# A buffer of its own for two kinds of working values, and a fifth slot in the shared pool

## The chip, the cores and the metric

The kernel runs on one core of one Trainium2 chip. A core has a matrix engine (TensorE, PE in the rows) and three engines for vectors, VectorE (DVE), ScalarE (ACT) and GpSimd (POOL); SyncE (SP) issues most of the loads. Each engine runs its own list of instructions in order; between engines semaphores order the work. Matrix products are written to PSUM, everything else lies in SBUF, the core's on-chip memory. The metric is the time of one execution on the device in microseconds: here 2623.21, the median of three runs (2622.59 to 2624.29).

## The reference, cut to what matters

Two decoder layers over 256 positions of width 2048, in f32. Layer 0 mixes latent attention (MLA) with a gated delta rule (GDN, 8 heads, chunks of 64 positions); layer 1 is a gated linear attention (GLA, 4 heads). After each mixer comes a SwiGLU feed-forward stage. Three pieces matter here:

```python
def rms_norm(x, gain):
    y = xf * lax.rsqrt(jnp.mean(xf * xf, axis=-1, keepdims=True) + EPS)
    return y * gain

# gated delta rule, per chunk of 64:
t_mat = jnp.eye(cs) + lower
sol = lax.linalg.triangular_solve(t_mat, rhs, left_side=True, lower=True, unit_diagonal=True)

# gated linear attention, per chunk of 64:
rel = jnp.exp(jnp.where(causal, b_c[:, :, :, None, :] - b_c[:, :, None, :, :], -jnp.inf))
scores = jnp.einsum('bhid,bhjd,bhijd->bhij', q_c, k_c, rel)
o = rms_norm(o, norm_g) * jax.nn.silu(r)
```

The modulation that stands around every stage is a product with a vector, `silu(c) @ ada_w`.

## The kernel before, in words

Activations are kept transposed: 16 tiles of 128 features by 256 positions (T = 256). Weights are loaded as f32 tiles `raw`; ScalarE casts each to `hi` (`L253`), VectorE subtracts to get `lo` (`L193`), and TensorE adds up products with both parts. These main products go to PSUM tiles `acc`, the small ones of the mixers to `sm`. Products for the modulation (`pa<-araw,sc`, VectorE's `ada`) are spread between them.

The stages in order: input projection with the convolution of the GDN (to about 320 us), MLA and GDN woven into each other (to 560), output projection (to 620), feed-forward 0 (to 1395), projections and heads of the GLA (to 1740), its output projection (to 1856), feed-forward 1 and the final norm. Python generators are woven (`weave`, `braid`) so that work of two kinds alternates in the program; a scheduler of the framework then fixes each engine's order, and a slot that is not free counts in it: an instruction is put where its slot is free. Which slot is free when thus decides the order of all engines.

The pool `tp` has these tags: `tmp`, working values of at most 128 x 512, 4 slots; `sv`, values of a few columns, 12 slots; `ss`, 1 slot, which holds the running sum of squares in `x_square`; `rs`, 1 slot. Those who use `tmp` are many: the steps of MLA and GDN, the squares, the tiles of `h_tile` at a stage's start, and the levels of the GLA.

Four pieces of the program are touched or stand next to what is touched.

`gdn_blocks` solves the 16 x 16 diagonal blocks of a half (4 heads) by substitution on GpSimd: 15 steps, each a product `w` and a subtraction. It then copies the result transposed (`L954`, ScalarE), stores both (`L956`) and loads them rearranged (`L959`). `gdn_local` stores each head's matrix with GpSimd DMAs (`L918`), which stand in the same order as the substitution. `gdn_merge` joins the blocks to 64 x 64, with small products on TensorE and, among others, the copies of `L1015`.

`rstd` gives 1 / rms: logarithm and exponential on ScalarE and a correction on VectorE, with two working values `w` and `y`. It serves the norms of MLA (`mla_rstd`), GDN (`gdn_tail`, 128 x 512), GLA (`gla_pv`), the stage norms (`x_rstd`) and the last one.

`gla_scores` computes a head's scores in eight levels (1 to 128). For each, `prepare` takes a `tmp` slot for the exponents `e` (two subtractions on VectorE, exp on ScalarE) and one for `ke` (product with k), and the product with q goes in place; `prepare` runs one level ahead. TensorE then multiplies the two (`sm<-tmp,tmp`). `gla_pv` multiplies by v, squares the four output tiles (a `tmp` slot each, ScalarE `L203`), sums them by products with ones (`sm<-tmp,cst`) and calls `rstd`.

`h_tile` makes a stage's input: a first step to `tmp` (`L200`), ScalarE's high part, and a second step that gives `d` (`L200`), which TensorE reads.

Of the kernel before, what the change touches and what calls it, by code (L numbers as in the profile page):

```python
# [9 lines left out]
F32 = mybir.dt.float32  # L10
# [9 lines left out]
T = 256  # L20
# [109 lines left out]
class Trunk:  # L130
# [29 lines left out]
        return s.dp.tile(list(shape), dt, tag="d", name=s.nm("d"))  # L160

    def tmp(s, shape=(128, 512), dt=F32):
        return s.tp.tile(list(shape), dt, tag="tmp", name=s.nm("tmp"))

    def sv(s, shape):
        return s.tp.tile(list(shape), F32, tag="sv", name=s.nm("sv"), bufs=12)
# [58 lines left out]

    def rstd(s, out, ss, n, eps=EPS):

        w = s.tmp(out.shape)
        y = s.tmp(out.shape)
        s.act(y, ss, AF.Ln, scale=1.0 / n, bias=s.eps[:out.shape[0]])  # L230
        s.ts(w, ss, -0.5 / n, ALU.mult, -0.5 * eps, ALU.add)
        s.act(y, y, AF.Exp, scale=-0.5)
        s.tt(w, w, y, ALU.mult)
        s.tt(w, w, y, ALU.mult)
        s.stt(out, w, 1.5, y, ALU.add, ALU.mult)
# [697 lines left out]
    def gdn_blocks(s, half):  # L933


        nc = s.nc
        lt = s.d((64, 16, 16))
        nc.gpsimd.dma_start(lt, s.lt[half].rearrange("u (b r) -> (u b) r", b=8)[:, :2048].rearrange(
            "l (j i) -> l j i", i=128)[:, :, :16])
        tr = s.d((64, 2, 16, 16))  # L940
        t = tr[:, 0]
        nc.gpsimd.memset(t, 0.0)
        nc.gpsimd.memset(t.rearrange("l i c -> l (i c)")[:, 0:256:17], 1.0)
        for _ in range(W0):
            yield
        for k in range(15):
            n, m = 15 - k, k + 1
            w = s.tmp((64, 16, 16))[:, :n, :m]
            s.tt(w, lt[:, k, m:].unsqueeze(2).broadcast_to([64, n, m]),
                 t[:, k, :m].unsqueeze(1).broadcast_to([64, n, m]), ALU.mult, nc.gpsimd if SG else None)  # L950
            s.tt(t[:, m:, :m], t[:, m:, :m], w, ALU.subtract, nc.gpsimd if SG else None)
            if k % SK == SK - 1:
                yield
        nc.scalar.copy(tr[:, 1], t.rearrange("l i c -> l c i"))  # L954
        blk = s.drp.tile([2, 64 * 256], F32, name=s.nm("blk"))
        nc.gpsimd.dma_start(blk.rearrange("a (l r) -> l a r", l=64), tr.rearrange("l a i c -> l a (i c)"))  # L956
        s.tc16[half] = s.d((128, 2, 8, 16))
        for a in range(2):
            nc.gpsimd.dma_start(s.tc16[half][:, a], blk[a].rearrange("(u b j i) -> (b j) u i", u=8, b=8, i=16))  # L959
        for _ in range(W1):  # L960
            yield
# [712 lines left out]
```

## Time and profile before

| quantity | value |
|---|---|
| median of three runs | 2623.21 us |
| the profiled execution | 2622.07 us |
| its span in the trace | 2620.3 us |
| TensorE busy | 2552.7 us (97%) |
| VectorE / ScalarE / GpSimd busy | 67% / 46% / 4% |
| mean granted clock of TensorE | 0.983 |
| chain of waits that ended last | TensorE 93%, VectorE 3%, ScalarE 1% |

Busy shares are means over the whole span. TensorE does not have a free share of 3% everywhere: the feed-forward stages have none, and what there is lies at the starts and ends of stages and in the mixers. The granted clock is 1.0 at 2.4 GHz and 0.5 at 1.2; work done at the lower takes about twice as long.

### The profile page before, as it was taken

What the parts mean: (1) busy time and instruction counts of PE and PEld (TensorE: products, weight loads), DVE (VectorE), ACT (ScalarE), POOL (GpSimd) and SP (SyncE); (2) the same over time, 40 slices, a digit from 0 to 9 for tenths busy, and PEclk for the clock granted to TensorE, in tenths of its full rate; (3) what the DMA queues carried; (4) which work ended last, traced back from release to release, by engine and by line L of the source; (5) the groups of instructions that cost most, each with busy time, mean ns of one, the idle gap of its engine ahead of it and who ended that gap; (6) DMA issues with size and microseconds to landing.
All of it is one profiled execution on the core that took longest, in us unless ns stands there. A gap on an engine that the chain in (4) does not pass through costs nothing.

```text
span 2620.3 us, 43320 instructions
## 1 busy us (share of the span) xinstructions
PE 2552.7 (97%) x17914; PEld 2285.0 (87%) x17914; DVE 1768.3 (67%) x2455; ACT 1193.8 (46%) x1809; POOL 97.6 (4%) x154
## 2 busy tenths in 40 slices
PE   8999998999999999999998989999999999999998
PEld 5799876799999999999998878878788888888887
DVE  3667654688778777777778777766655655655555
ACT  3435664445433343334345534564544344444344
POOL 0000014001000000000001000001000000000001
PEclk9999998899999999999999999999999999999999
DMA  9975567675979888878885545435455555555553
GB/s 349 351 290 167 212 251 255 261 286 205 341 276 352 310 312 313 323 298 324 308 326 191 203 166 197 166 120 193 161 190 186 189 191 190 182 191 193 177 193 113
DMA packets 262259, 622.31 MB, mean 237 GB/s; under 512 B 17119, under 2 KB 28012, under 8 KB 241582
## 3 DMA queue, kind: packets, MB, share of 16 engines
q1 hardware_dynamic: 259902, 608.32, 65.5%
q0 software_dynamic: 1968, 11.14, 1.2%
q8 instruction: 141, 2.31, 0.3%
q14 instruction: 56, 0.46, 0.0%
q10 hardware_dynamic: 192, 0.08, 0.0%
HBM read 616.09 MB, written 3.41 MB: 236 GB/s over the span
## 4 chain that ended last, share of the span: by engine, by line
PE 93%; DVE 3%; ACT 1%; DMA 1%; issue 1%; POOL 0%; SPq 0%; DVEq 0%; ACTq 0%; POOLq 0%
PE acc L190 85%; PE sm L190 5%; PE pa L190 2%; DVE lo L193 1%; ACT hi L253 1%; DMA araw<-in_ada_w 0%; DVE ada L200 0%; DVE tmp L193 0%; ACT tmp L203 0%; DVE d L193 0%; DMA d<-in_x 0%; POOL ss L193 0%; DMA d<-in_ada_w 0%; DMA d<-in_norm_g 0%; DVE x L200 0%
## 5 line engine op out<-in xcount | busy, mean ns | idle before, releaser
L190 PE MATMUL acc<-d,hi 128*128 128x256 f32 (+2 forms) x9120 | 2138.9, 321 | 16.4 <-DVE d L200 9.2
L190 PE MATMUL acc<-d,lo 128*128 128x256 f32 x6000 | 1642.8, 283 | 3.2 <-DVE lo L193 3.2
L190 PEld LDWEIGHTS acc<-d,hi 128*128 128x128 f32 (+1 forms) x9120 | 1500.7, 191 | 164.7 <-issue 20.6
L193 DVE TENSOR_TENSOR lo<-raw,hi 128x1024 fp32r<-128x1024 f32 (+2 forms) x801 | 945.2, 1204 | 576.1 <-ACT hi L253 560.6
L253 ACT CAST hi<-raw 128x1024 fp32r<-128x1024 f32 x776 | 786.0, 1047 | 991.6 <-PE acc L190 845.9
L190 PEld LDWEIGHTS acc<-d,lo 128*128 128x128 f32 x6000 | 1138.5, 191 | 30.9 <-DVE lo L193 5.4
L200 DVE SCALAR_TENSOR_TENSOR ada<-araw,sc,ada 128x1024 f32<-128x1024 f32 x240 | 299.8, 1287 | 6.3 <-DMA araw<-in_ada_w 6.2
L200 DVE SCALAR_TENSOR_TENSOR x<-acc,mod,x 128x256 f32<-128x256 f32 x272 | 119.8, 478 | 42.5 <-PE acc L190 41.6
L193 DVE TENSOR_TENSOR d<-acc,d 128x256 f32<-128x256 f32 (+1 forms) x200 | 93.2, 474 | 74.1 <-PE acc L190 52.0
L190 PE MATMUL acc<-hi,d 128*128 128x512 f32 (+1 forms) x320 | 96.0, 379 | 1.3 <-DVE d L193 1.3
L190 PE MATMUL pa<-araw,sc 128*32 128x512 f32 x480 | 75.5, 631 | 3.4 <-DMA araw<-in_ada_w 2.0
L223 ACT CAST d<-d 128x256 fp32r<-128x256 f32 x128 | 48.3, 405 | 53.2 <-DVE d L193 53.1
L193 DVE TENSOR_TENSOR d<-d,d 128x256 fp32r<-128x256 f32 (+1 forms) x155 | 61.2, 420 | 12.0 <-ACT d L223 8.2
L190 PEld LDWEIGHTS acc<-hi,d 128*128 128x128 f32 x320 | 58.5, 191 | 12.4 <-DVE d L193 1.4
L190 PE MATMUL acc<-lo,d 128*128 128x512 f32 (+1 forms) x160 | 59.8, 373 | 0.0
L203 ACT ACTIVATE d<-d 128x256 f32<-128x256 f32 (+1 forms) x94 | 45.5, 489 | 26.4 <-DVE d L200 11.6
L193 POOL TENSOR_TENSOR ss<-ss,tmp 128x256 f32<-128x256 f32 x44 | 49.1, 1115 | 72.1 <-ACT tmp L203 70.2
L193 DVE TENSOR_TENSOR tmp<-d,tmp 128x512 f32<-128x512 f32 x64 | 43.9, 687 | 10.0 <-ACT tmp L203 3.9
L514 POOL COPY ss<-tmp 128x256 f32<-128x256 f32 x3 | 2.6, 880 | 1009.5 <-ACT tmp L203 1009.5
L280 ACT COPY d<-acc 128x256 f32<-128x256 f32 x76 | 27.6, 370 | 26.5 <-PE acc L190 25.3
L203 ACT ACTIVATE d<-tmp,mod 128x256 fp32r<-128x256 f32 x64 | 29.2, 502 | 21.6 <-DVE tmp L200 16.6
L190 PEld LDWEIGHTS sm<-tmp,tmp 128*128 128x128 f32 x240 | 31.8, 193 | 8.1 <-issue 6.4
(215 smaller groups left out, 1100.1 us busy)
## 6 DMA issues: line engine op xcount, KB each, us to landing
raw<-in_ffn_w SPq DMA_DIRECT2D x264, 1024.0 KB, 5.1
araw<-in_ada_w SPq DMA_DIRECT2D x175, 1024.0 KB, 7.2
raw<-in_gla_w_in SPq DMA_DIRECT2D x48, 1024.0 KB, 5.1
raw<-in_ab_w_in SPq DMA_DIRECT2D x30, 1024.0 KB, 4.9
raw<-in_ab_w_out SPq DMA_DIRECT2D x16, 1024.0 KB, 5.3
raw<-in_gla_w_out SPq DMA_DIRECT2D x16, 1024.0 KB, 5.1
raw<-in_ab_w_in SPq DMA_DIRECT2D x20, 512.0 KB, 7.5
araw<-in_ada_w POOLq DMA_DIRECT2D x9, 1024.0 KB, 5.1
```

Of the source, the lines that this page charges most:

```text
L190: s.nc.tensor.matmul(out, lhsT=lhsT, rhs=rhs, start=start, stop=stop)
L193: (eng or s.nc.vector).tensor_tensor(out=out, in0=a, in1=b, op=op)
L200: return s.nc.vector.scalar_tensor_tensor(out=out, in0=a, scalar=sc, in1=b, op0=op0, op1=op1)
L203: s.nc.scalar.activation(out, a, f, **kw)
L223: s.nc.scalar.copy(hl[:, 0], x)
L253: s.nc.scalar.copy(hi[:, :n, :ncol], raw[:, a:a + n, :ncol])
L280: s.nc.scalar.copy(out, ps[:, T:])
L514: s.nc.gpsimd.tensor_copy(s.ss, q)
```

## The change

The pool tag `tmp` gets five slots. The substitution's product `w` takes the one slot of `ss`. In `rstd`, values of T columns put `w` in `ss` and `y` in the output itself; values of up to 8 columns put both in `sv`; the 512-column ones of `gdn_tail` stay with `tmp`. The instructions are the same, but for three loads of ScalarE's function tables (32 before, 29 now).

```diff
     def tmp(s, shape=(128, 512), dt=F32):
-        return s.tp.tile(list(shape), dt, tag="tmp", name=s.nm("tmp"))
+        return s.tp.tile(list(shape), dt, tag="tmp", name=s.nm("tmp"), bufs=5)
+
+    def row(s, shape=(128, T)):
+        return s.tp.tile(list(shape), F32, tag="ss", name=s.nm("ss"), bufs=1)
...
     def rstd(s, out, ss, n, eps=EPS):
 
-        w = s.tmp(out.shape)
-        y = s.tmp(out.shape)
+        n1 = out.shape[-1]
+        w = s.sv(out.shape) if n1 <= 8 else s.row() if n1 == T else s.tmp(out.shape)
+        y = out if n1 == T else s.sv(out.shape) if n1 <= 8 else s.tmp(out.shape)
         s.act(y, ss, AF.Ln, scale=1.0 / n, bias=s.eps[:out.shape[0]])
...
         for k in range(15):
             n, m = 15 - k, k + 1
-            w = s.tmp((64, 16, 16))[:, :n, :m]
+            w = s.row((64, 16, 16))[:, :n, :m]
```

The order of the instructions moves with it, on all engines. Three places follow, each first as it stands before and then as it stands now (lines of the code are 3 or 4 higher now, and the numbers behind names differ by a few).

GpSimd, the last steps of the first half's substitution. `lt` is the DMA that stores a head's matrix; `blk` and the last row are the way of the result. Before:

```order
L193 TENSOR_TENSOR d_4003<-d_4003,tmp_4281 64x3x13
L193 TENSOR_TENSOR tmp_4284<-d_4001,d_4003 64x2x14
L193 TENSOR_TENSOR d_4003<-d_4003,tmp_4284 64x2x14
L193 TENSOR_TENSOR tmp_4287<-d_4001,d_4003 64x15
L918 DMA lt_3935<-d_4314 128x2x128
L193 TENSOR_TENSOR d_4003<-d_4003,tmp_4287 64x15
L956 DMA blk_4346<-d_4003 64x2x256
L959 DMA d_4348<-blk_4346 128x8x16 x2
```

The same steps of GpSimd now, with `ss` in place of `tmp`:

```order
L196 TENSOR_TENSOR d_4001<-d_4001,ss_4279 64x3x13
L196 TENSOR_TENSOR ss_4282<-d_3999,d_4001 64x2x14
L922 DMA lt_3933<-d_4185 128x2x128
L196 TENSOR_TENSOR d_4001<-d_4001,ss_4282 64x2x14
L196 TENSOR_TENSOR ss_4285<-d_3999,d_4001 64x15
L196 TENSOR_TENSOR d_4001<-d_4001,ss_4285 64x15
L960 DMA blk_4344<-d_4001 64x2x256
L963 DMA d_4346<-blk_4344 128x8x16 x2
L922 DMA lt_3933<-d_4312 128x2x128
```

The products are written to `ss`; the store that stood ahead of the last subtraction has gone behind the two DMAs of the result, and the store before it, which stood six steps from the end, stands two steps from it.

ScalarE in the second half. The copy from `d` to `d`, 64 x 256, is the transposed copy of the substitution's result; `tmp<-sm`, 32 x 128 are the copies that TensorE's merge needs. Before:

```order
L1019 COPY d_4447<-d_4442 32x4x32 x2
L1017 COPY d_4445<-d_4442 32x4x32 x4
L1015 COPY tmp_4748<-sm_4739 32x128 x2
L1250 COPY tmp_4761<-acc_4757 128x384
L954 COPY d_4411<-d_4411 64x256
L203 ACTIVATE d_4429<-sm_4798 32x4x32
```

The same stretch of ScalarE now:

```order
L1023 COPY d_4445<-d_4440 32x4x32 x2
L1021 COPY d_4443<-d_4440 32x4x32 x4
L958 COPY d_4409<-d_4409 64x256
L1019 COPY tmp_4746<-sm_4737 32x128 x2
L1254 COPY tmp_4759<-acc_4755 128x384
L1254 COPY tmp_4769<-acc_4765 128x384
L1019 COPY tmp_4780<-sm_4771 32x128 x2
```

The transposed copy has moved from behind the first pair of merge copies to in front of it.

TensorE in the last levels of GLA head 0. `sm<-tmp,tmp` are the products of a level, `acc` the main products. Before:

```order
L190 MATMUL acc_16340<-d_15576,lo_16533 128x256
L190 MATMUL acc_16340<-d_15576,hi_16532 128x512
L190 MATMUL sm_16403<-tmp_16367,tmp_16371 128x128 x4
L190 MATMUL sm_16452<-tmp_16396,tmp_16400 128x128 x4
L190 MATMUL sm_16484<-tmp_16445,tmp_16449 128x128 x2
L190 MATMUL sm_16512<-cst_85,d_15858 128x128
L190 MATMUL sm_16512<-cst_85,d_15866 128x128
L190 MATMUL sm_16512<-cst_85,d_15858 128x128
L190 MATMUL sm_16512<-cst_85,d_15866 128x128
L190 MATMUL sm_16520<-d_15755,d_16061 128x128 x4
L190 MATMUL sm_16536<-cst_85,tmp_15421 128x4 x4
L190 MATMUL acc_16607<-hi_16611,d_15501 128x512
```

TensorE now, around the second last level's products and then around the last level's:

```order
L193 MATMUL acc_16335<-d_15552,lo_16469 128x256
L193 MATMUL acc_16335<-d_15552,hi_16468 128x512
L193 MATMUL sm_16448<-tmp_16392,tmp_16396 128x128 x4
L193 MATMUL acc_16336<-d_15537,lo_16465 128x256
```

On either side of the second last level stand main products. The last level:

```order
L193 MATMUL acc_16333<-d_15567,lo_16529 128x256
L193 MATMUL acc_16333<-d_15567,hi_16528 128x512
L193 MATMUL acc_16333<-d_15572,lo_16529 128x256
L193 MATMUL sm_16480<-tmp_16441,tmp_16445 128x128 x2
L193 MATMUL sm_16508<-cst_85,d_15854 128x128
L193 MATMUL sm_16508<-cst_85,d_15862 128x128
L193 MATMUL sm_16508<-cst_85,d_15854 128x128
L193 MATMUL sm_16508<-cst_85,d_15862 128x128
L193 MATMUL sm_16516<-d_15751,d_16057 128x128 x4
L193 MATMUL acc_16333<-d_15572,hi_16528 128x512
```

Before, three levels and the small products behind them stand in one piece. Now main products stand between: 36 between the third last and the second last of these groups, 15 between the second last and the last, and 25 among and behind the small ones.

ScalarE near the end of the last heads. The copies `d<-sm` bring an output tile, the activation `tmp<-d` squares it, `L280` copies carry gate tiles; the pair of activations between table loads is the logarithm and exponential of 1 / rms. Before:

```order
L203 ACT_TABLE_LOAD
L203 ACTIVATE tmp_18096<-sm_17949,eps_105 128x256
L203 ACT_TABLE_LOAD
L203 ACTIVATE tmp_18096<-tmp_18096 128x256
L1488 COPY d_18119<-sm_18122 128x256
L280 COPY d_18156<-acc_17966 128x256
L280 COPY d_18156<-acc_17967 128x256
L1488 COPY d_18119<-sm_18169 128x256
L280 COPY d_18184<-acc_17968 128x256
L280 COPY d_18184<-acc_17969 128x256
L203 ACTIVATE tmp_18126<-d_18119 128x256
L203 ACTIVATE tmp_18173<-d_18119 128x256
```

The same stretch of ScalarE now:

```order
L206 ACT_TABLE_LOAD
L206 ACTIVATE d_18088<-sm_17943,eps_105 128x256
L206 ACT_TABLE_LOAD
L206 ACTIVATE d_18088<-d_18088 128x256
L1492 COPY d_18112<-sm_18115 128x256
L206 ACTIVATE tmp_18119<-d_18112 128x256
L257 CAST hi_18203<-raw_18201 128x1024
L257 CAST hi_18207<-raw_18201 128x1024
L284 COPY d_18149<-acc_17960 128x256
L284 COPY d_18149<-acc_17961 128x256
L1492 COPY d_18112<-sm_18162 128x256
L206 ACTIVATE tmp_18166<-d_18112 128x256
```

The first square has moved from behind six copies to right behind the first one; the output of 1 / rms is its own working value.

## Rows read from the trace of the kernel before

**Rows 1.** The page, part 1: busy time and share of the span.

```profile
...
PE 2552.7 (97%) x17914; PEld 2285.0 (87%) x17914; DVE 1768.3 (67%) x2455; ACT 1193.8 (46%) x1809; POOL 97.6 (4%) x154
```

**Rows 2.** TensorE's waits: for which engine and line, us in total, times, longest.

```profile
...
PE sm L190 <- ACT tmp L203: 8.8, 5, 4.7
PE sm L190 <- DVE tmp L193: 6.0, 2, 4.2
...
```

**Rows 3.** Timeline of GpSimd in both halves: start, us, operation, [idle before <-releaser].

```profile
...
401.76 0.75 POOL L918 DMA_DIRECT2D lt<-d  x1 [1.38 <-DVE d L193]
...
428.33 0.78 POOL L193 TENSOR_TENSOR tmp<-d,d 64x63 f32<-64x63 f32 x1 [3.33 <-PE acc L1248]
429.19 1.18 POOL L193 TENSOR_TENSOR d<-d,tmp 64x63 f32<-64x63 f32 x1
...
434.58 1.14 POOL L193 TENSOR_TENSOR tmp<-d,d 64x55 f32<-64x55 f32 x1
...
438.45 0.21 POOL L193 TENSOR_TENSOR d<-d,tmp 64x15 f32<-64x15 f32 x1
...
```

**Rows 4.** Timelines of ScalarE and TensorE at the merge of the second half.

```profile
...
437.49 0.54 ACT L1015 COPY tmp<-sm 32x128 f32<-32x128 f32 x2 [3.00 <-POOL d L193]
...
438.69 0.62 ACT L954 COPY d<-d 64x256 f32<-64x256 f32 x1
...
437.80 0.47 PE L190 MATMUL sm<-tmp,d 32*32 32x32 f32 x5 [4.75 <-ACT tmp L1015]
...
```

**Rows 5.** Windows: us, busy PE, PEld, DVE, ACT, POOL; PEclk; DMA share; GB/s.

```profile
...
437.00:447.00 10.00, 8.10 (x51) 5.54 (x52) 3.13 (x5) 5.41 (x16) 3.74 (x9) 0.50 1.02 403
...
1522.00:1529.00 7.00, 5.13 (x27) 4.95 (x26) 2.39 (x5) 1.02 (x3) 0.00 (x0) 0.53 0.41 147
...
1731.00:1738.00 7.00, 6.12 (x20) 5.24 (x21) 4.78 (x13) 5.04 (x11) 0.00 (x0) 0.54 0.18 71
...
```

**Rows 6.** Line 959's issues and landings, and TensorE's transposes for attention.

```profile
...
L959 POOL DMA_DIRECT2D d<-blk x4: 892/915/942, 407.6 to 445.5; - x4
...
DMA to landing us min/median/max: 4.0/5.3/7.5
...
410.02 0.44 PE L1248 MATMUL acc<-cst,tmp 128*128 128x128 f32 x2
...
```

**Rows 7.** Timeline of TensorE in the last levels of GLA head 0.

```profile
...
1515.62 0.39 PE L190 MATMUL acc<-d,hi 128*128 128x512 f32 x1
1515.85 0.28 PE L190 MATMUL acc<-d,lo 128*128 128x256 f32 x1
1515.97 0.39 PE L190 MATMUL acc<-d,hi 128*128 128x512 f32 x1
...
1521.40 1.16 PE L190 MATMUL sm<-tmp,tmp 128*128 128x128 f32 x8 [4.16 <-DVE tmp L193]
1524.43 1.19 PE L190 MATMUL sm<-tmp,tmp 128*128 128x128 f32 x4 [1.87 <-DVE tmp L193]
...
1531.25 0.50 PE L190 MATMUL acc<-hi,d 128*128 128x512 f32 x1 [1.29 <-DVE d L193]
...
```

**Rows 8.** The page, part 5: the casts to `lo` (count, busy, mean ns).

```profile
...
L193 DVE TENSOR_TENSOR lo<-raw,hi 128x1024 fp32r<-128x1024 f32 (+2 forms) x801 | 945.2, 1204 | 576.1 <-ACT hi L253 560.6
...
```

**Rows 9.** Timelines of ScalarE and TensorE at the end of the last heads.

```profile
...
1727.68 0.47 ACT L203 ACTIVATE tmp<-sm,eps 128x256 f32<-128x256 f32 x1
...
1729.79 0.35 ACT L1488 COPY d<-sm 128x256 f32<-128x256 f32 x1
...
1731.36 0.77 ACT L203 ACTIVATE tmp<-d 128x256 f32<-128x256 f32 x2
...
1731.88 1.22 PE L190 MATMUL sm<-tmp,cst 128*128 128x256 f32 x2 [4.68 <-ACT tmp L203]
...
```

**Rows 10.** Timelines of VectorE and TensorE at the start of feed-forward 1.

```profile
...
1858.11 1.67 DVE L200 SCALAR_TENSOR_TENSOR tmp<-x,mod,rs 128x256 f32<-128x256 f32 x4
...
1860.32 0.76 PE L190 MATMUL acc<-d,hi 128*128 128x512 f32 x1 [4.84 <-DVE d L200]
...
```

## The prediction

> **What bounds the kernel now.** I began with the page's first part and the chain of waits: TensorE is busy for 97% of the span, so nearly every step of the chain that ended last is one of its matmuls [rows 1]. Both feed-forward stages are matmuls without a hole, so the change has nothing to win there. What it can win is the idle time of TensorE, 2620.3 - 2552.7 = 67.6 us, and time at half clock. The waits of TensorE come second: 8.8 us are waits for `tmp` from ScalarE's line 203 and 6.0 for `tmp` from VectorE's line 193 [rows 2]. Both name the pool that gets a fifth slot. I then read the timelines around the long waits and, last, windows of the granted clock over what follows each of them.
>
> Four places matter: the substitution of the delta rule (387 to 447 us), the levels of head 0 of the gated linear attention (GLA; about 1495 to 1532), the end of its last heads (1726 to 1738), and the stage boundaries near 622, 1406 and 1858.
>
> **The substitution.** The change moves its 30 products (15 per half) from `tmp` to the one `ss` slot. That slot has no other user in this stage, and product and subtraction alternate on GpSimd, which runs in order, so one slot is enough. In the first half nothing waited for a slot; what it lost there are DMA issues that stand between its steps or just ahead of it: the one at 401.76 alone waited 1.38 us and took 0.75 [rows 3]. In the new order this one stands behind the substitution and the two before it stand behind further steps, so this half ends 2.1 us sooner from the one, and by my estimate up to 4 with the others. In the second half a product waited 3.33 us for a `tmp` slot that TensorE was still reading [rows 3]. That wait goes: the end moves from 438.66 (438.45 + 0.21) to 435.3. TensorE's wait of 4.75 us hangs on this: ScalarE's two copies of line 1015 needed a `tmp` slot that GpSimd's products held until 437.49 [rows 4]. They no longer need it, but in the new order the transposed copy of the whole half (line 954, 0.62 us [rows 4]) stands in front of them, and this one waits for the last subtraction. So the copies start at about 435.3 + 0.7 = 436.0 instead of 437.49, and TensorE at 436.3 instead of 437.80: 1.5 us gained.
>
> How fast the products run bounds this from the other side. Their subtractions and products of some 0.3 us took 1.18 us at 429.19 and 1.14 at 434.58 [rows 3], the first and the last of four slow ones; they cost about 4 x 0.85 = 3.4 us. Freed of these too, the half would end at 431.9 and the wait of 4.75 would be gone almost whole, and with it up to 4 us at half clock (437 to 447: 8.10 us of work at 0.50 [rows 5], half of it lost), 8.8 in all. The Trainium skill, page "GPSIMD Engine Reference", section "1. Specifications", says that GpSimd shares its SBUF interfaces with VectorE and contends with VectorE's instructions that have two SBUF inputs. By that rule the slow steps are not slow by their place and come again wherever VectorE's casts run, so the gain stays at the low end, 1.5; without it, it could be 4.75 and more. I take 2.0, near the low end, because VectorE has the same long operations to do between 426 and 436, and I leave the clock as it is: a wait of about 3 us stays, and the stretches behind waits of 1.87 and 4.68 us are granted 0.53 and 0.54 [rows 5, 7, 9], near the lower of the two levels, 1.2 of 2.4 GHz.
>
> A loss belongs to the same place. TensorE's first merge step of the first head pair moves ahead of attention's transposes that stood at 410.02. It needs the blocks that the line 959 DMAs bring: first issued at 407.6, 4.0 to 7.5 us to land, 5.3 in the median [rows 6]. With the substitution 2.1 to 4 us earlier they land between 407.6 and 413.0, so TensorE waits 0 to 3.0 us there. With the median it is 408.9 to 410.8, at most 0.8, and I take 0.8.
>
> **Head 0 of the GLA.** TensorE waits 4.16, 1.87 and 1.29 us for its last levels, 7.3 us together [rows 7], with nothing between them. Each level takes two slots (the exponent and k times it) and is prepared one level ahead, so four slots are all in use and a level's preparation starts when TensorE has read an older one; meanwhile VectorE and ScalarE have worked off casts, the `lo` casts of 1.20 us [rows 8] among them, in the middle of the chain. In the new order the level steps come ahead of later casts, and TensorE gets main matmuls between the levels: 36 ahead of the second last group, 15 ahead of the last, 25 around the small products behind it. Starts are 0.23 us apart behind a wide one and 0.12 behind a narrow one [rows 7], so these are 36 x 0.175 = 6.3, 2.6 and 4.4 us of work for waits of 4.16, 1.87 and 1.29. The second is not quite safe: two `lo` casts (2 x 1.20 us) now stand between the two steps on VectorE. I count 1.5 us as remaining and 0.8 for what the interleaving loses elsewhere: 5.0 gained. At half clock 1522 to 1529 holds 5.13 us of work at 0.53 [rows 5], about 2.4 us lost; I take 1.5 back. Term: 6.5, bounds 0 (the level chain is as long as before and the filler only moves) and 7.3 + 2.4 = 9.7, more if the dip behind it goes too.
>
> **The last heads.** TensorE waits 4.68 us at 1731.88 for a square [rows 9]. ScalarE does the logarithm at 1727.68, the exponential with table loads between, copies from 1729.79 on and only then the square, at 1731.36 [rows 9]: the squares have to wait until 1 / rms, whose two working values and the four squares share four slots, gives some back. With the working value in `ss`, the result in place and five slots, the square stands right behind the first copy, and TensorE has 32 main matmuls between the former square's product and this one: 16 x 0.23 + 16 x 0.12 = 5.6 us. ScalarE needs 1729.79 + 0.35 - 1727.68 = 2.5 us to the end of the first copy and about 0.4 for the square, so the wait can vanish. I take 3.5 of the 4.68, as other waits of the same chain follow (product, rms, gate, output matmul), and 1.5 of the 2.8 that 6.12 us of work at 0.54 lose [rows 5]. Term: 5.0, bounds 0 and 7.5.
>
> **The boundaries.** With a fifth slot one more first step (`tmp` from `x`) goes ahead of the first second step (`d` from `tmp`) on VectorE at the three boundaries. Four take 1.67 us at 1858.11, 0.40 each, and the wait of 4.84 at 1860.32 ends with the first `d` [rows 10]. Each boundary so loses 0.4: -1.2 together. The other edits (1 / rms of the 8-wide values in `sv`, the in-place result at the boundaries, three table loads fewer on ScalarE, which is idle for more than half the span) are at nothing: VectorE's own chain is as long as before, and matmuls cover the rest.
>
> **Sum.** 2.0 - 0.8 + 6.5 + 5.0 - 1.2 = 11.5 us. The profiled execution took 2622.07 us (span 2620.3), 1.1 below the median; from the median the sum gives 2623.21 - 11.5 = 2611.7 us. All terms at their best: 8.8 + 9.7 + 7.5 - 1.2 = 24.8, 2598.4; all at their worst: 1.5 - 3.0 + 0 + 0 - 1.2 = -2.7, 2625.9.
>
> **Rivals.**
> *The waits move, they do not go* (0.22). The chains of levels and of 1 / rms are as long as before, and TensorE meets the same chain with its main matmuls in another place. For it: in the substitution the new copy in front of line 1015 does just that. Against: in the old order TensorE has no main matmul at all between the last levels. A third of the three gains is 13.5 / 3 - 2 = 2.5 us; when one of the two GLA places gains in full it is 6 to 7: 2616 to 2621, the middle 2619.
> *`tmp` was not the limit* (0.08). The slots come free when wanted and only names change: 2623. Against it stands the 3.33 us wait for a slot.
> *Casts too late* (0.15). In the new order level steps and squares stand ahead of hi and lo casts on in-order engines, and TensorE then starves for weights. A pair of `lo` casts costs 2 x 1.20 = 2.4 us when TensorE arrives before it. If this happens at six pairs in the GLA stage, it is 14.4 us, and with one further stretch at half clock (7 us, half lost) 17.9: 17.9 - 11.5 = 6.4 slower, 2629.6. It decides from five pairs on. For it: two casts now stand between the steps of the second last level. Against: over the whole stage VectorE and ScalarE are far from full, and hi and lo have four slots each.
>
> **Numbers.** Forecast 0.55, rivals 0.22, 0.08, 0.15. A difference of 0.2% (5.2 us) is about what can be told from no change here. Of the forecast 0.53 is faster; of the first rival 0.09 faster and 0.13 the same; the second is the same, 0.08; of the third 0.14 is slower and 0.01 the same. Faster 0.62, same 0.24, slower 0.14. The range is 2602 to 2625: below it are the cases with nearly all best terms, above it most of the third rival.
>
> **What would show it.** Right: no wait of GpSimd for a slot in the second half, its end near 435; TensorE's wait for line 1015's copies at 2 to 3.5 us; in head 0 and in the last heads no wait of TensorE over 2 us, and the stretches of 7 us behind these waits with a granted clock well above the 0.53 and 0.54 of before; boundary waits of 4.7 and 5.2 us. Wrong: a wait of several us for the merge step near 410, or waits for `lo` or `hi` in the GLA stage.

## The result, and the profile after

The changed kernel takes 2592.01 us (median of 4 runs, 2590.08 to 2595.17) against 2623.47 (4 runs, 2622.59 to 2624.29): ratio 0.9881, 95% interval 0.9864 to 0.9898, 31.5 us faster. The forecast was 11.5 us. The direction was right, the size was not, and the time lies far below the stated range.

The profiled execution took 2593.56 us, its span is 2591.4. TensorE's own part of the page:

```profile
...
PE 2538.1 (98%) x17914; PEld 2279.1 (88%) x17914; DVE 1769.3 (68%) x2455; ACT 1188.7 (46%) x1806; POOL 99.0 (4%) x154
...
```

Of the 28.9 us of span, idle time of TensorE makes 67.6 - 53.3 = 14.3, and its busy time 2552.7 - 2538.1 = 14.6 [rows 1]. TensorE's instructions are the same, so the second half is work that went faster. The waits of TensorE in the changed kernel, in the columns of [rows 2]:

```profile
...
PE acc L193 <- DVE d L203: 9.8, 2, 5.1
PE sm L193 <- ACT tmp L206: 3.9, 3, 2.3
...
PE sm L193 <- ACT tmp L1019: 3.2, 1, 3.2
...
```

The waits for VectorE's `tmp`, 6.0 us before, are no longer in the list; those for ScalarE's `tmp` fell from 8.8 to 3.9. To see where the time came from I cut both traces at the same instructions of TensorE and took for each stage its length, TensorE's idle time in it, and the work done while the granted clock was at half (worked out from the records of TensorE and of the clock; us):

| stage (us of before) | before: length, idle, work at half clock | changed | its second profile (e8) |
|---|---|---|---|
| start, 0 to 125 | 121.7, 11.7, 13.7 | 120.5, 12.1, 6.7 | 121.7, 11.9, 12.7 |
| convolution, MLA, delta rule, 125 to 640 | 515.0, 13.7, 27.4 | 505.6, 10.7, 24.7 | 504.7, 12.0, 19.5 |
| start of GLA, 1380 to 1415 | 35.0, 7.0, 5.2 | 34.5, 7.4, 4.1 | 34.6, 7.3, 4.5 |
| GLA with head 0, 1415 to 1690 | 275.0, 8.5, 8.4 | 265.2, 0.0, 3.4 | 263.8, 0.0, 0.0 |
| last heads, 1690 to 1760 | 70.2, 4.7, 5.5 | 60.8, 0.0, 0.0 | 60.8, 0.0, 0.0 |
| start of feed-forward 1, 1850 to 1870 | 20.0, 5.3, 3.4 | 21.1, 5.6, 5.2 | 20.1, 5.6, 3.2 |

The two GLA stages give 9.8 + 9.4 = 19.2 us and the delta rule stage 9.4. Of the 19.2 us, 13.2 are idle time and 5.2 the clock (half of the 13.9 - 3.4 us of work at half clock). How they divide at 1690 is less sure: 16 level products (`sm<-tmp,tmp`, some 1.8 us) stand ahead of this cut in the new order and stood behind it before, so that head 0 gained about 11.6 and the last heads about 7.6. What the places of the prediction look like now, in the order of its terms:

GpSimd's timeline in both halves, in the columns of [rows 3]:

```profile
...
381.65 0.21 POOL L196 TENSOR_TENSOR ss<-d,d 64x15 f32<-64x15 f32 x1 [3.68 <-DMA d<-lt]
...
384.13 0.75 POOL L922 DMA_DIRECT2D lt<-d  x1
...
395.06 0.21 POOL L196 TENSOR_TENSOR d<-d,ss 64x15 f32<-64x15 f32 x1
...
410.97 0.53 POOL L994 MEMSET d<- 128x512 f32 x1 [5.09 <-DVE d L196]
411.46 0.21 POOL L196 TENSOR_TENSOR ss<-d,d 64x15 f32<-64x15 f32 x1
...
427.26 1.12 POOL L196 TENSOR_TENSOR d<-d,ss 64x15 f32<-64x15 f32 x1
...
```

No step waits for a slot. The second half ends at 428.4 instead of 438.7, 10 us sooner and not 3.3: it starts at 411.46 where it began at 420.84 before. The kernel before in the same places:

```profile
...
386.55 0.72 POOL L918 DMA_DIRECT2D lt<-d  x1 [3.44 <-DVE d L193]
387.37 0.23 POOL L193 TENSOR_TENSOR tmp<-d,d 64x15 f32<-64x15 f32 x1
...
402.53 0.23 POOL L193 TENSOR_TENSOR d<-d,tmp 64x15 f32<-64x15 f32 x1
...
420.09 0.53 POOL L990 MEMSET d<- 128x512 f32 x1 [8.68 <-PE acc L190]
...
420.84 0.21 POOL L193 TENSOR_TENSOR tmp<-d,d 64x15 f32<-64x15 f32 x1
...
```

ScalarE and TensorE at the merge, as in [rows 4]:

```profile
...
427.12 1.22 ACT L1021 COPY d<-d 32x128 f32<-32x128 f32 x4
428.41 0.62 ACT L958 COPY d<-d 64x256 f32<-64x256 f32 x1
429.06 0.54 ACT L1019 COPY tmp<-sm 32x128 f32<-32x128 f32 x2
...
```

```profile
...
429.37 0.47 PE L193 MATMUL sm<-tmp,d 32*32 32x32 f32 x5 [3.20 <-ACT tmp L1019]
...
```

TensorE still waits 3.20 us, within the 2 to 3.5 that the prediction gave. Near 410 it does not wait at all. Windows over the places, as in [rows 5]:

```profile
...
429.00:436.00 7.00, 6.63 (x50) 5.99 (x51) 0.57 (x2) 2.19 (x8) 0.64 (x1) 0.52 1.00 391
439.00:449.00 10.00, 9.97 (x61) 7.65 (x61) 3.21 (x9) 3.43 (x13) 0.77 (x2) 0.51 0.61 213
1495.00:1525.00 30.00, 30.00 (x177) 26.44 (x176) 26.70 (x45) 14.80 (x22) 0.53 (x1) 1.00 0.56 184
1690.00:1712.00 22.00, 22.00 (x126) 19.36 (x126) 15.53 (x24) 16.38 (x27) 0.00 (x0) 1.00 0.47 154
...
```

In the third row lie the last levels of head 0, in the fourth the last heads: TensorE is busy without a hole and the clock is 1.00, where it was 0.53 and 0.54 behind the waits. The last levels themselves, as in [rows 7]:

```profile
...
1500.83 1.05 PE L193 MATMUL sm<-tmp,tmp 128*128 128x128 f32 x8
...
1504.27 0.61 PE L193 MATMUL sm<-tmp,tmp 128*128 128x128 f32 x4
...
```

Neither row has a wait in brackets. ScalarE in the last heads, as in [rows 9]:

```profile
...
1695.02 0.48 ACT L206 ACTIVATE d<-sm,eps 128x256 f32<-128x256 f32 x1 [0.97 <-PE sm L193]
...
1697.13 0.35 ACT L1492 COPY d<-sm 128x256 f32<-128x256 f32 x1
1697.52 0.42 ACT L206 ACTIVATE tmp<-d 128x256 f32<-128x256 f32 x1
...
```

From the logarithm to the end of the first square are 2.9 us, as worked out, and TensorE has main products for them. At the boundary the wait grew as forecast, from 4.84 to 5.13 [rows 10]:

```profile
...
1830.04 0.76 PE L193 MATMUL acc<-d,hi 128*128 128x512 f32 x1 [5.13 <-DVE d L203]
...
```

### The profile page after: what moved, and what is told of

It is laid out like the page before. It is cut to its first block, busy times and chain, and to the rows that moved or that the text cites. A ratio compares the mean times of both kernels' runs of the same rounds, so it can differ in the third digit from the quotient of the medians.

```text
span 2591.4 us, 43280 instructions
## 1 busy us (share of the span) xinstructions
PE 2538.1 (98%) x17914; PEld 2279.1 (88%) x17914; DVE 1769.3 (68%) x2455; ACT 1188.7 (46%) x1806; POOL 99.0 (4%) x154
## 4 chain that ended last, share of the span: by engine, by line
PE 94%; DVE 2%; ACT 1%; issue 1%; DMA 1%; POOL 1%; SPq 0%; DVEq 0%; ACTq 0%; POOLq 0%
PE acc L193 86%; PE sm L193 5%; PE pa L193 2%; DVE lo L196 1%; ACT hi L257 1%; POOL ss L196 0%; DVE ada L203 0%; DMA d<-in_x 0%; DMA raw<-in_ab_w_in 0%; DVE tmp L203 0%; DMA araw<-in_ada_w 0%; POOL d L196 0%; DVE x L203 0%; ACT tmp L206 0%; DVE d L196 0%
## 5 line engine op out<-in xcount | busy, mean ns | idle before, releaser
L193 PE MATMUL pa<-araw,sc 128*32 128x512 f32 x480 | 70.6, 617 | 4.1 <-DMA araw<-in_ada_w 2.7
L196 POOL TENSOR_TENSOR ss<-ss,tmp 128x256 f32<-128x256 f32 x44 | 48.3, 1097 | 72.3 <-ACT tmp L206 70.3
L206 ACT ACTIVATE d<-tmp,mod 128x256 fp32r<-128x256 f32 x64 | 28.8, 501 | 19.8 <-DVE tmp L203 14.3
L193 PEld LDWEIGHTS sm<-d,d 32*32 32x32 f32 (+2 forms) x368 | 29.8, 146 | 9.2 <-issue 5.9
## 6 DMA issues: line engine op xcount, KB each, us to landing
raw<-in_ab_w_in SPq DMA_DIRECT2D x20, 512.0 KB, 7.9
```

The costliest lines, as they stand in the source:

```text
L193: s.nc.tensor.matmul(out, lhsT=lhsT, rhs=rhs, start=start, stop=stop)
L196: (eng or s.nc.vector).tensor_tensor(out=out, in0=a, in1=b, op=op)
L206: s.nc.scalar.activation(out, a, f, **kw)
```

## The experiments

Theory A: each part pays at its own place: the fifth slot at head 0 of the GLA, 1 / rms at the last heads, products (with 1 / rms) in the delta rule. Theory B: slots are slots, and any that come free give the whole gain. Theory C: the gain is luck of the whole order. Times are medians; each is compared with the kernel before on the same chip: 2620.17 for the first four, 2619.27 for the next four, 2619.22 for the last three.

**The parts alone.** e1 has only the fifth slot, e2 only the products, e3 only 1 / rms, e4 the last two without the slot.

```diff
 e1
-        return s.tp.tile(list(shape), dt, tag="tmp", name=s.nm("tmp"))
+        return s.tp.tile(list(shape), dt, tag="tmp", name=s.nm("tmp"), bufs=5)
 e2
-            w = s.tmp((64, 16, 16))[:, :n, :m]
+            w = s.row((64, 16, 16))[:, :n, :m]
 e3
+        w = s.sv(out.shape) if n1 <= 8 else s.row() if n1 == T else s.tmp(out.shape)
+        y = out if n1 == T else s.sv(out.shape) if n1 <= 8 else s.tmp(out.shape)
```

> Alone of the change: tmp with five slots; products and working values of 1 / rms stay in tmp. Theory A (each part pays at its own place: the fifth slot at the levels of GLA head 0, 1 / rms at the end of the last heads, products and 1 / rms together in the delta rule): its order on TensorE has main matmuls between the last levels of head 0 (36 and 15) and, by the fifth slot, also 38 ahead of the squares' product of the last heads, so the GLA stage (1408 to 1855 before) is shorter by 17 to 20 us; the delta rule stage, where GpSimd's stores stand as before, by 0 to 3: about 2602. Theory B (any slot that comes free is as good as any other, since one pool serves all): 2592 to 2596, all of the 31 us. Theory C (the gain is the scheduler's luck with the whole order): the stages that change do not answer to the places; 2592 to 2623.

> Alone of the change: the substitution's products in the ss slot; four tmp slots, 1 / rms as before. Theory A: GLA as before to 0.5 us, its waits of 4.2, 1.9, 1.3 and 4.7 us and its half clock unchanged; in the delta rule stage GpSimd's wait of 3.3 us for a slot is gone and TensorE's wait of 4.75 us for the line 1015 copies shrinks (the copies stand ahead of the transposed copy here), but the store that held back the first half still stands in front of it: 3 to 6 us, about 2619. Theory B: 2592 to 2610. Theory C: a change of several us in GLA too.

> Alone of the change: the working values of 1 / rms out of tmp; four slots, products in tmp. Theory A: the waits at head 0 stay (no main matmul between its last levels in this order), the wait of 4.7 us at the last heads goes with its half clock (25 main matmuls ahead of that product): 8 us; in the delta rule stage the first store stands six rows later, so the first half is earlier by 3 to 5, but the wait for a slot in the second half stays: 0 to 4 us. About 2612. Theory B: 2592 to 2600. Theory C: 2600 to 2623.

> All of the change but the fifth slot. Theory A: the waits and the half clock of head 0 stay (11 us that the changed kernel saved), the last heads (8 us) and the delta rule stage (9 us) gain as in the changed kernel: 2604 to 2606. Theory B: 2592 to 2597, since products and working values no longer take slots and four are enough. Theory C: no relation to the places.

| run | us, ratio (95%) | 125 to 640: length, idle, work at half clock | 1415 to 1690 | 1690 to 1760 |
|---|---|---|---|---|
| before | - | 515.0, 13.7, 27.4 | 275.0 | 70.2 |
| e1 slot | 2603.80, 0.9943 (0.9927 to 0.9960) | 514.7, 13.7, 20.4 | 263.7 | 60.7 |
| e2 products | 2611.41, 0.9964 (0.9952 to 0.9976) | 500.6, 8.0, 5.5 | 278.3 | 70.3 |
| e3 1 / rms | 2611.12, 0.9964 (0.9952 to 0.9976) | 512.0, 14.4, 28.1 | 277.7 | 61.7 |
| e4 both | 2619.28, 0.9991 (0.9982 to 0.9999) | 512.2, 9.1, 33.1 | 277.7 | 60.8 |

In GLA this is Theory A, with one correction. Head 0's stage is shorter by 11 us with the fifth slot and not at all without it; the products leave its waits as they were (in e2 TensorE's waits there are 4.16 and 1.86), though its stage is 3.3 us longer in e2, with 17.6 us of work at half clock for 8.4 before. The last heads gain 8.5 to 9.5 with the slot alone or with 1 / rms alone: either is enough, so of the change one would have done there. That the GLA stages answer to the parts speaks against C there; e1 with 16.4 of 31.5 us speaks against B (its runs reach from 2600.14 us, at a granted clock of 0.990, to 2612.70, at 0.986).

In the delta rule stage the parts do not add up, and two expectations failed by it: e2 came out 8 us below the 2619 expected, e4 13 us above 2604 to 2606. The products alone save 14.4 us there, more than the whole change; with 1 / rms besides (e4) only 2.8. The difference is mainly the clock. In e2, ScalarE's merge copies come before the end of the substitution, TensorE's wait is 0.64 us instead of 4.75, and the clock stays full; e4 has a stretch at half clock of 25 us:

```profile
...
420.00:450.00 30.00, 29.27 (x378) 21.43 (x379) 16.26 (x33) 18.39 (x55) 15.93 (x38) 1.00 0.81 299
...
```

```profile
...
451.00:476.00 25.00, 24.39 (x238) 16.00 (x238) 10.13 (x21) 6.48 (x21) 0.00 (x0) 0.52 0.49 177
...
```

The first row is e2, the second e4; in [rows 5] the same stage of before had 0.50 over 10 us. Of e4's 12 runs (2612.05 to 2621.95) the profiled one is the fastest, so its median is 7 us above what the table accounts for. The granted clock over the whole run was 0.985 in the profiled one and 0.981 to 0.983 in the nine from 2616.93 us up; 0.002 to 0.004 of 2612 us are 10 to 21 us more at half clock, so by this estimate 5 to 10 us. The 7 us are thus most likely clock; in which stages they lie no trace shows.

**Pairs, and the changed kernel again.** e5 is the change without 1 / rms, e6 without the products (their diffs are those above, undone); e8 is the changed kernel itself.

> The change without its part in 1 / rms: five tmp slots and the products in ss. By theory A (each part at its place) with what the runs of the single parts showed: delta rule stage 14 us shorter than before, as with the products alone (its order there has the copies of the merge ahead of the transposed copy, like that run's), head 0 of GLA 11 and last heads 9 shorter, as with the fifth slot alone, boundaries 1 longer: 2586 to 2590, faster than the changed kernel. If the part in 1 / rms is needed for the last heads: 2595 to 2600. If the delta rule stage is luck of the order: 2590 to 2605.

> The change without the products: five slots, 1 / rms out of tmp, products in tmp. Theory A: GLA as in the changed kernel (its order there is nearly the same), 20 us shorter than before; the delta rule stage 0 to 4 us, as with 1 / rms alone or the fifth slot alone: about 2600. If products matter beyond their place: GLA differs from the changed kernel by more than 2 us.

> The changed kernel again, on the same chip as the three others: 2588 to 2595, and where the clock was halved in this execution compared with the first one, to see which dips belong to the program and which to the run. Theory A expects the dips behind waits of over 2 us again (429, 610, 1395, 1830) and those early in the program to come and go.

Measured: e5 2596.56 (0.9925, 0.9909 to 0.9940; 2595.29 to 2608.56), e6 2596.33 (0.9911, 0.9898 to 0.9924), e8 2592.55 (0.9900, 0.9886 to 0.9915). In both pairs GLA is as in the changed kernel to 2 us (263.4 and 60.7; 265.0 and 60.8). e6's delta rule stage gained 5.1 us, where 0 to 4 were expected. The expectation for e5 failed: the 14 us of the products alone did not come again, its delta rule stage gained 7.6 (idle 8.4, work at half clock 18.6). So what a single part gives there holds for its order only. e8's dips (stretches at half clock) are those of the first profile behind its waits at 429, 610, 1395 and 1828, while the ones in the first 125 us differ (work at half clock 6.7 and 12.7). So does the stretch from 439 to 449, granted 0.51 in the first profile and 1.00 in e8; neither has a wait of over 0.4 us between 431 and 460. Those belong to the run, not to the program.

**The clock by itself.** e7 is the kernel before with extra matmuls where TensorE waits, 20 near the end of head 0's levels and 8 ahead of the last head's sum of squares. They write what is overwritten later; nothing of the chains is removed, though the order around them moves.

```diff
+            for _ in range({64: 14, 128: 6}.get(lv, 0) if hh == 0 else 0):
+                s.mm(ps[:, 0:128], k[:, 0, 0:128], q[:, 0, 0:128])
...
         def norm(e):
+            for _ in range(8 if hh == 3 and e == 0 else 0):
+                s.mm(pss[:, :T], s.c("ones"), s.gq[hh][:, 0])
```

> The kernel before with extra matmuls whose results are overwritten, put where TensorE waits: 20 of 128 x 128 x 128 behind the third last level of GLA head 0 (some 5 us) and 8 of 128 x 256 ahead of the first sum of squares of the last head (some 4 us). The chains that are waited for stay. If the clock falls because TensorE is idle there, the waits shrink in name only, the stretches 1522 to 1536 and 1731 to 1737 run at full clock, and the time is 4 + 3 = 7 us less than before: 2613. If the granted clock falls for another reason, the time is that of before or up to 5 us more, 2620 to 2625. If both, the wait and the clock, had been needed for the gain of the changed kernel, this kernel has about 40% of its 20 us in GLA.

Measured: 2614.98 us (0.9976, 0.9966 to 0.9987; seven runs from 2610.43 to 2617.36), 4.3 us faster by the median although TensorE has more to do. The first fence shows its head 0 on TensorE, the second windows over head 0 and over the last heads (columns as in [rows 5]); the profiled execution took 2614.98 us:

```profile
...
1517.47 4.63 PE L190 MATMUL sm<-d,d 128*128 128x128 f32 x40
...
1522.83 1.06 PE L190 MATMUL sm<-tmp,tmp 128*128 128x128 f32 x8
...
```

```profile
...
1500.00:1540.00 40.00, 39.52 (x251) 35.30 (x250) 31.86 (x53) 17.06 (x24) 0.53 (x1) 1.00 0.45 146
1716.00:1734.00 18.00, 16.54 (x90) 14.50 (x89) 8.58 (x18) 12.21 (x24) 0.00 (x0) 1.00 0.33 113
...
```

The row of 4.63 us is throwaway work where the wait of 4.16 was; the level's own product starts at 1522.83, where it started at 1521.40 before, so the chain of levels up to it has not become shorter. The clock is 1.00 in both windows. From the first main product of the GLA (1407.93 before) to the last products of squares ahead of feed-forward 1 (1854.79) the kernel before takes 446.9 us, e7 437.3 and the changed kernel 426.6. Of e7's 9.6 us, 7.3 are the clock's part: its work at half clock fell from 19.1 us to 4.6. The other 2.2 are idle time that went: it fell from 13.3 to 3.3 us, while the throwaway work took 7.8 (TensorE's busy time compared, with the half clock taken out). In e7's order the small products behind the last levels stand between them, and the waits of 1.87 and 1.29 are gone. The 20.3 us that the change gains over the same stretch are 13.1 of idle time, 5.8 of clock and 1.4 of neither.

**What the remaining waits cost, and a faster version.** e9 is the changed kernel with extra matmuls behind the last sum of squares of three stages (4, 9 and 9), e10 has 6 more ahead of the merge step that waits 3.2 us. e11 moves the substitution's transposed copy from ScalarE to GpSimd.

```diff
 e9 (in x_rstd; s.lastq is the last square)
+        n = s.nfill.pop(0)
+        if n:
+            pf = s.sm()
+            for _ in range(n):
+                s.mm(pf[:, :T], s.c("ones"), s.lastq)
 e10 (in gdn_merge)
+            for _ in range(6 if p == 0 else 0):
+                s.mm(pz[:, 2:4].rearrange("p a u i -> p (a u i)"), s.c("ones"), s.c("gmask"))
 e11
-        nc.scalar.copy(tr[:, 1], t.rearrange("l i c -> l c i"))
+        nc.gpsimd.tensor_copy(tr[:, 1], t.rearrange("l i c -> l c i"))
```

> The changed kernel with extra matmuls (128 x 128 x 256, their result read by nobody) where TensorE waits at the starts of feed-forward 0 (4), GLA (9) and feed-forward 1 (9); nothing else. If idle time of TensorE is what lowers the clock: the waits of 4.6 and 5.1 us are shorter by some 4 us in name, the half clock behind them (6.8 us each, 3 to 5 us of work in each) is gone, and 4 to 7 us are saved against the changed kernel: 2586 to 2588. If the dips there have another cause: 2592 or up to 3 more.

> The same and 6 such matmuls ahead of the merge step that waits 3.2 us for the line 1019 copies in the delta rule stage. If that wait alone causes the half clock from 429 to 449: 4 to 8 us more are saved, 2579 to 2583. If the second dip there (439 to 449, behind no wait of over 0.3 us) has its own cause: 2 to 4 more, 2583 to 2586.

> The changed kernel with the substitution's transposed copy on GpSimd instead of ScalarE, so that it no longer stands in front of the merge copies of ScalarE. If the step of the prediction holds (the merge copies are tied to the end of the substitution by that copy): ScalarE's copies start some 2 us sooner, TensorE's wait of 3.2 us is under 1.5 and the delta rule stage 2 to 6 us shorter: 2586 to 2590. If the merge copies wait for something else: as the changed kernel to 2 us, 2590 to 2594.

e9: 2587.94 us (0.9876, 0.9860 to 0.9893), e10: 2584.88 (0.9869, 0.9852 to 0.9885), the fastest of all, 7.7 us below e8. e9 is as its first theory expected, 2586 to 2588. e10 is 3.1 us below e9, where its first theory expected 4 to 8: it lies in the range of the second, 2583 to 2586. In e9 the waits for VectorE's first `d` are 0.37 us at the start of the GLA and none at feed-forward 1, and the clock is 1.00 behind both; at feed-forward 0 four extra matmuls left 1.43 of 2.14 us and a clock of 0.67 over 610 to 620. In e10 the dip at 429 (0.52 in the changed kernel, 0.53 in e8) is gone with the wait ahead of it. The one at 439 (0.51) is gone too, but e8 lacks it with the wait in place, so that it hung on this wait is not shown. e10's merge step, and a window over both places:

```profile
...
425.89 2.86 PE L193 MATMUL sm<-cst 128*128 128x256 f32 x12
...
429.63 0.34 PE L193 MATMUL sm<-tmp,d 32*32 32x32 f32 x5 [0.56 <-ACT tmp L1026]
...
```

```profile
...
429.00:449.00 20.00, 19.17 (x188) 15.50 (x191) 10.78 (x22) 10.14 (x31) 4.03 (x7) 1.00 0.74 269
...
```

e11: 2592.25 us (0.9893, 0.9876 to 0.9909), the same as the changed kernel. The substitution ended at 423.6 with its copy on GpSimd, 4.8 us sooner than in the changed kernel, and ScalarE's merge copies still came late:

```profile
...
423.25 1.05 ACT L257 CAST hi<-raw 128x1024 fp32r<-128x1024 f32 x1 [2.31 <-PE acc L193]
...
428.72 1.22 ACT L1021 COPY d<-d 32x128 f32<-32x128 f32 x4
429.96 0.54 ACT L1019 COPY tmp<-sm 32x128 f32<-32x128 f32 x2
...
```

From 423.25 on ScalarE works without a pause (two casts, two exponentials and small copies) until the merge copies at 429.96. TensorE's wait is 2.52 us instead of 3.20. So the transposed copy costs about its own 0.62 us and no more; what holds the merge copies is ScalarE's own list in front of them.

## Why the prediction was wrong

Of the 17.4 us by which the span gained more than the 11.5 forecast, 8.2 lie in the stage of the substitution and 7.7 in the two GLA terms.

**The terms of head 0 and the last heads: right mechanism, sizes too small.** The step that failed is the discount. For head 0 the prediction counted 7.3 us of waits and 2.4 of clock, and took 6.5; for the last heads 4.68 and 2.8, and took 5.0, "as other waits of the same chain follow". They did not: both stages run without idle time. Counted were 12.0 us of waits and 5.2 of clock, gained 13.2 and 5.2, of 19.2 in all; taken were 8.5 and 3.0. That the main products between the levels fill the waits was read off the order rightly (36, 15 and 25), and e1 shows that the fifth slot alone brings it. The clock was taken back by 1.5 + 1.5 us, while e7 shows that the clock's part in GLA is 7.3 us there, and that filling the idle time is enough to get it back. The bounds stood in the text, 9.7 and 7.5. The last heads reached theirs (about 7.6); head 0 with about 11.6 passed it, since 1.2 us more of idle time went from its stage than the three waits that were counted.

**The term of the substitution, 2.0 - 0.8: 9.4 measured.** Three steps of it failed, and one of the paragraph on the boundaries.

First, "the end moves from 438.66 (438.45 + 0.21) to 435.3" assumed that the second half starts where it did. It started 9.4 us sooner, and the first half ended 7.5 us sooner (395.3 for 402.8). Of these 7.5, TensorE was 4.5 ahead already at 380 us: 1.2 from the first 125 us, where e8 has nothing of it, and some 3.4 from 125 to 380. The steps themselves took 13.6 us for 15.4, about the 2.1 that the prediction gave to the store at 401.76. The store of the fifth head, which had waited 3.44 us ahead of the first product, stands behind eight of the products and subtractions now (384.13), but the first product waits 3.68 us for a load in its place. Ahead of the second half stands a memset that waited for TensorE before (8.68 us) and for VectorE now (5.09); how much of the 9.4 us comes from the first half is not shown.

Second, that the transposed copy "stands in front of them, and this one waits for the last subtraction" is true in the order but is not what sets the wait (e11): it is ScalarE's casts and small copies. The forecast of the wait, 2 to 3.5 us, was met for another reason, by luck.

Third, "I leave the clock as it is": its half-clock work fell from 27.4 to 24.7 and 19.5 us in the two profiles, 1.4 and 4 us gained, and 3.0 and 1.7 us are idle time. The rest, some 5 us, is neither: it is TensorE's work that became cheaper.

That leads to the step of the other paragraph: the other edits, 1 / rms among them, "are at nothing", since "matmuls cover the rest". Between the same two main products, at 320 and 380 us before, TensorE has no idle time and takes 60.1 or 60.2 us in the kernel before, e1, e2 and e5 (in e7 59.9, with its half clock taken out), and 56.5 or 56.6 in all eight profiles with the part in 1 / rms. So this part is worth 3.6 us here (last section). The remaining 1.5 us of cheaper work stay open, and so does which edit brings the idle time and the clock of this stage, as its parts do not add up. The wait for the blocks near 410, taken as 0.8, did not come.

**The boundaries, -1.2:** 4.84 became 5.13 and 4.32 became 4.65: 0.3 each, close to the 0.4 taken; at feed-forward 0, 2.05 became 2.14. **The speed of a step:** slow steps came again in the second half, six of 1.09 to 1.38 us for four before. GpSimd's first two and VectorE's instruction beside them, in the changed kernel:

```profile
...
418.05 1.38 POOL L196 TENSOR_TENSOR ss<-d,d 64x63 f32<-64x63 f32 x1
419.52 1.19 POOL L196 TENSOR_TENSOR d<-d,ss 64x63 f32<-64x63 f32 x1
...
```

```profile
...
418.00 2.52 DVE L203 SCALAR_TENSOR_TENSOR ada<-araw,sc,ada 128x1024 f32<-128x1024 f32 x2
...
```

The other four lie in the same way beside VectorE's two `lo` casts (422.74 and 424.69, 1.23 us each) and the next such pair (425.83, 2.48 us); the half's other 24 steps take 0.21 to 0.32 us. That agrees with what the Trainium skill, page "GPSIMD Engine Reference", section "1. Specifications", says of the shared interfaces, and the steps were not slow by their place. The prediction stayed low for that reason, rightly for the speed; the gain came from elsewhere.

**The rivals.** "Casts too late" did not happen: the waits of TensorE for `lo` are 3.2 us in both profiles, and all of them early in the program. "The waits move": in the delta rule in part. e3 has as much idle time there as before (14.4 for 13.7); e4 has 9.1 but 33.1 us of work at half clock for 27.4. In GLA they do not move.

## What to carry to other kernels

A wait of an engine that bounds the kernel costs itself and what the clock does behind it; here the change gained 13.1 us of idle time in GLA and 5.8 of clock. Filling the waits of two places there with work that is thrown away gave 9.6 us back, 7.3 of them clock, and filling others 7.7 us on top of the change (e10 against e8). When a new order puts main work into a wait, count the whole wait with its clock unless a wait that can be pointed to in the new order takes its place. An edit that moves slots also moves the order of work that waits for nothing, so its term is not nothing: 3.6 us here. Where several parts meet in one stage of woven work, test the pairs: the best single part (14 us) was not additive there, while in GLA head 0 needs the slot and the last heads either part.

## What the runs showed of the hardware that was not expected

The small products for the modulation, `pa`, cost by runs, not by number. Two rows of the kernel before, eight of them in a row and four:

```profile
...
405.58 1.06 PE L190 MATMUL pa<-araw,sc 128*32 128x512 f32 x8
...
406.83 1.05 PE L190 MATMUL pa<-araw,sc 128*32 128x512 f32 x4
...
```

Eight take as long as four. Over the whole trace of before, four to eight in a row take 0.98 to 1.00 us until TensorE's next instruction, twelve to sixteen 1.84 to 1.85 (medians, at full clock). So the order decides what they cost by how it groups them. Between the two main products at 320 and 380 us the kernel before has nine groups (60 products, 10.6 us), and the changed kernel, like each of the eight profiles with the part in 1 / rms, five (54 products, in groups of 18, 6, 14, 8 and 8; 7.5 us): 3.1 of the 3.6 us by which this stretch is shorter. No run changed the grouping by itself. The 480 of the whole program are busy for 75.5 us before and 70.6 in the changed kernel:

```profile
...
L193 PE MATMUL pa<-araw,sc 128*32 128x512 f32 x480 | 70.6, 617 | 4.1 <-DMA araw<-in_ada_w 2.7
...
```

Of these 4.9 us about 2.6 are the clock: five groups of eight were at half clock before and two are now, at 1.86 us each instead of 1.00.

Second, the delta rule stage was granted 0.52, the lower level, over 25 us in e4, while TensorE had matmuls for 24.4 of them; ahead of it stands a wait of 2.21 us at 450.79. What ends such a stretch was not tried, nor why the one from 439 to 449 comes in one run of the changed kernel and not in the next.
